# A hybrid decoder trunk on one core: the state-space mixer's tables, its input products and its accumulators

## The chip, the cores and the metric

The kernel runs on one core of a Trainium2 chip. The metric is the device time of one execution in microseconds (us). Engines are named as in the profile: PE is TensorE (PEld its weight loads), DVE is VectorE, ACT is ScalarE, POOL is GpSimd, SP is SyncE, which issues most of the DMAs.

## The reference

The input is x, 256 tokens of width 2048, in float32. Two layers follow each other, and each is a mixer and a gated MLP with a causal convolution of width 3, both behind an RMSNorm and both added to the residual. Layer 0's mixer is a chunked spatial gate. Layer 1's mixer, which the change touches, is a diagonal complex state-space model:

```
u = (rms_norm(h) @ b_w_in)                  # 128 heads of 16 channels
h_t = A h_(t-1) + B u_t ;  y_t = Re(C h_t) + d * u_t      # A diagonal, complex, 64 states a head
ga, gb = split(gelu(y) @ b_w_glu) ;  h = h + ga * sigmoid(gb)
```

## The kernel before

All large products are float32 split in two halves (wh and wl), three products for each. A weight tile (1 MB) is fetched by SP (L108) into one of three raw buffers, cut in pieces of 1024 columns, cast by ACT (wh, L124) and subtracted by DVE (wl, L125) into five buffers each. PE takes them in the order of the list of tiles. Accumulators (acc, accb) come from a PSUM pool of three buffers of two banks each; a second pool, misc, has two buffers of one bank for everything else. Together they fill PSUM.

The scheduler sets the order on each engine by a simulated timeline: it takes, at the time at which the engine is free in it, the instruction earliest in the program among those whose inputs are there. On the chip every engine then runs its instructions in that order, and waits where an input is late. SP does so for its DMAs too.

The mixer's stage lies from about 1046 to 1376 us. PE first makes u = h W (form_a, L786 and L787), eight groups of 256 channels with two weight tiles each, then the GLU's products (group_b, L893 to L895). Between the tiles a step of a software pipeline is put in (step, called once a tile), which takes 16 sets s of eight heads through the state space:

- evac of a group (L1207, L1209, L1213): ACT copies half of acc to t, DVE adds, scales and turns it to u; SP writes u to DRAM (send, L543).
- load and load1, one step ahead of the drive: SP fetches u back as ubd, two blocks of 64 partitions on the diagonal of a tile that is zero elsewhere (L551), the drive's weights pw (L556) and the phase tables tab (cos and sin, 2 x 512 columns, L566). Both halves of tab, partitions 0 to 63 and 64 to 127, hold the same rows of DRAM and are fetched twice.
- drive (L584): four matmuls of 128 x 128 columns, from pw and ubd, into ps_x, a misc buffer.
- take (L597 to L600): ACT copies ps_x crosswise to x, DVE multiplies by the tables. scan (L608 to L610): the recurrence on DVE. turn (L620 to L625): back with the tables, to sp.
- outputs (L639, L645): matmuls on two column tiles of 64, into ps_y. gelu (L653) on ACT, then SP writes y (L655); POOL fetches it as yt (L661); finish casts it (L1168, L1169) to the GLU's stationary operand.

A set's steps come at fixed slots (N_OF): 3, 4, 6 to 14 without a gap, then every second slot up to 24. At slot n the drive, at n + 1 take and scan, at n + 2 turn, at n + 3 outputs.

A pool's memory is given to the next pool when it closes (SBUF: L527, L531 and L534 are the first writes of the mixer's pool).

Of the kernel before, what the change touches and what calls it, by code (L numbers as in the profile page):

```python
# [9 lines left out]
F32 = mybir.dt.float32  # L10
# [3 lines left out]
ALU = mybir.AluOpType  # L14
PSUM = bass.MemoryType.PSUM
DRAM = bass.MemoryType.DRAM

P = 128
# [13 lines left out]
def dram(ap, offset, dims):  # L32
    return bass.AP(ap.tensor, ap.offset + offset, dims)
# [41 lines left out]
class Weights:  # L75


    def __init__(self, nc, pool, tiles):
        self.nc, self.pool, self.tiles = nc, pool, tiles
        self.raw, self.halves = {}, {}  # L80
        self.n_dma = self.n_split = self.n_get = 0
        self.units = []
        for i, (segs, nk, width) in enumerate(tiles):
            for o in range(0, nk * width, 1024):
                self.units.append((i, o, min(1024, nk * width - o)))
        self.first_unit = {}
        for u, (i, o, n) in enumerate(self.units):
            self.first_unit.setdefault(i, u)
# [428 lines left out]
class S5Tokens:  # L517


    def __init__(self, tc, pool, psum, scr, rho, emit):  # L520
        self.nc, self.pool, self.psum = tc.nc, pool, psum
        self.scr, self.rho, self.emit = scr, rho, emit
        self.u, self.st = {}, {}
        self.ubd, self.sp = [], []
        for i in range(4):
            t = pool.tile([P, 4, P], F32, name=f"ubd{i}", tag=f"ubd{i}")
            self.nc.gpsimd.memset(t, 0.0)  # L527
            self.ubd.append(t)
        for i in range(2):
            t = pool.tile([P, 8, 64], F32, name=f"sp{i}", tag=f"sp{i}")  # L530
            self.nc.gpsimd.memset(t, 0.0)  # L531
            self.sp.append(t)
        self.rt = pool.tile([P, 8, 64], F32, name="rt")
        self.nc.gpsimd.memset(self.rt, 0.0)  # L534
# [24 lines left out]
    def load1(self, s):  # L559

        rd = self.scr[3]
        tab = self.pool.tile([P, 2, 512], F32, name=f"tab{s}", tag="tab", bufs=3)
        lh = 8 * s % 64
        o = ((lh // 16) * P + 64 * (s // 8)) * 2048 + (lh % 16) * 64
        for i in range(2):
            self.nc.sync.dma_start(tab[64 * i : 64 * i + 64], dram(rd, o, [[2048, 64], [1024, 2], [1, 512]]))  # L566
        self.st[s]["tab"] = tab

    def load2(self, s):
# [9 lines left out]
    def drive(self, s):  # L579

        st = self.st[s]
        st["x"] = self.psum.tile([P, 512], F32, name=f"ps_x{s}", tag="misc")
        for i in range(4):
            self.nc.tensor.matmul(  # L584
                st["x"][:, i * P : (i + 1) * P], st["pw"][:, i, :], st["ubd"][:, i, :], start=True, stop=True
            )

    def take(self, s):

        nc, pool = self.nc, self.pool  # L590
        V, A = nc.vector, nc.scalar
        st = self.st[s]
        ps = st["x"]
        q = pool.tile([P, 512], F32, name=f"q{s}", tag="q", bufs=2)
        x = pool.tile([P, 512], F32, name=f"x{s}", tag="x", bufs=2)
        cos, sin = st["tab"][:, 0, :], st["tab"][:, 1, :]
        A.copy(x[0:64], ps[64:128])  # L597
        A.mul(x[64:128], ps[0:64], -1.0)
        V.tensor_tensor(q, ps, cos, op=ALU.mult)
        V.tensor_tensor(x, x, sin, op=ALU.mult)  # L600
        st["q"], st["dx"] = q, x

# [66 lines left out]
def tile_hybrid_trunk(  # L669
# [7 lines left out]
    V, A, T, G = nc.vector, nc.scalar, nc.tensor, nc.gpsimd  # L677
# [2 lines left out]
    const = ctx.enter_context(tc.tile_pool(name="const", bufs=1))  # L680
    dpool = ctx.enter_context(tc.tile_pool(name="scratch", bufs=1, space=DRAM))
    wpool = ctx.enter_context(tc.tile_pool(name="weights", bufs=1))
    acc_ps = ctx.enter_context(tc.tile_pool(name="acc_ps", bufs=3, space=PSUM))
    misc_ps = ctx.enter_context(tc.tile_pool(name="misc_ps", bufs=2, space=PSUM))


    def ffn_groups(l):
# [52 lines left out]
    rho = const.tile([P, NH], F32, name="rho")  # L740
# [6 lines left out]
    scr = []  # L747
# [156 lines left out]
    def group_b(*args):  # L904
        for _ in group_b_steps(*args):
            pass
# [101 lines left out]
    with ExitStack() as sgu_ctx:  # L1008
        sp = sgu_ctx.enter_context(tc.tile_pool(name="sgu", bufs=1))
# [69 lines left out]
        for g in range(4):  # L1079
            st = {}  # L1080
# [77 lines left out]


    tmp[0] = ("t", 1)  # L1160
    with tc.tile_pool(name="s5", bufs=1) as sp:

        Ys = [None] * KC

        def emit(s, yt):
            g, yv = Gt[s], yt.rearrange("p (j k) -> p k j", j=4)
            hi, lo = (g[:, i * NT : (i + 1) * NT].rearrange("p (k j) -> p k j", j=4) for i in range(2))
            A.copy(hi, yv)  # L1168
            V.tensor_tensor(lo, yv, hi.bitcast(F32), op=ALU.subtract)  # L1169
            Ys[s] = g  # L1170

        s5 = S5Tokens(tc, sp, misc_ps, scr, rho, emit)
        rbv = rbc.rearrange("p (k j) -> p j k", j=4)
        sched = {}

        def at(slot, fn, *a):
            sched.setdefault(slot, []).append((fn, a))

        for s in range(KC):
            n = N_OF[s]  # L1180
            at(n - 1, s5.load, s)
            at(n - 1, s5.load1, s)
            at(n, s5.drive, s)
            at(n + 1, s5.take, s)
            at(n + 1, s5.scan, s)
            at(n + 1, s5.load2, s)
            at(n + 2, s5.turn, s)
            at(n + 3, s5.outputs, s)
            at(n + 4, s5.gelu, s)
            at(n + LAT[0], s5.fetch, s)  # L1190
            at(n + LAT[1], s5.finish, s)
        order = (
            s5.gelu, s5.take, s5.finish, s5.fetch, s5.turn, s5.scan, s5.outputs, s5.drive, s5.load2, s5.load, s5.load1
        )

        n_slot = [0]

        def step():
            for fn, a in sorted(sched.pop(n_slot[0], []), key=lambda e: order.index(e[0])):
                fn(*a)  # L1200
            n_slot[0] += 1

        for gi in range(8):

            def evac(p, ps, gi=gi):
                t = sp.tile([P, 2, NT], F32, name="t", tag="t", bufs=tmp[0][1])
                A.copy(t, ps[:, :, NT:])  # L1207
                z = sp.tile([P, 2, NT], F32, name="z", tag="z", bufs=2)
                V.tensor_tensor(z, ps[:, :, :NT], t, op=ALU.add)  # L1209
                for i in range(2):  # L1210
                    s = 2 * gi + i
                    u = s5.new_u(s)
                    V.tensor_tensor(u, z[:, i].rearrange("p (k j) -> p j k", j=4), rbv, op=ALU.mult)  # L1213
                    s5.send(s)

            after = {i: step for i in range(2)}
            if gi == 0:
                after[0] = lambda: (drain(2), make_rbc(sp), step())
            form_a(X, [8, 8], [0, 128], evac, after)

        kept = {}

        def glu_keep(i):


            def evac(ps):
                kept[i] = [const.tile([P, 512], F32, name=f"kept{i + a}", tag=f"X{i + a}", bufs=1) for a in range(2)]
                for a in range(2):
                    A.copy(kept[i][a], ps[:, a, :])

            return evac

        def glu_evac(i):
            def evac(ps):
                for a in range(2):
                    z = sp.tile([P, 512], F32, name="z", tag="z", bufs=2)
                    V.tensor_tensor(z, ps[:, a, :], kept[i][a], op=ALU.add)
                    A.activation(z[:, NT:], z[:, NT:], AF.Sigmoid)
                    V.tensor_tensor(z[:, :NT], z[:, :NT], z[:, NT:], op=ALU.mult)
                    hv = hn[:, a, i * P : (i + 2) * P]  # L1240
                    V.tensor_tensor(hv, hv, z[:, :NT], op=ALU.add)
                    square_sum(sp, hv, nss[:, a, i // 2 : i // 2 + 1])
                pending.append(lambda: stage_pair(i // 2, cols[:, 3]))
                if i == KC - 2:
                    total_r(nss, 8, rtok)

            return evac

        fa = group_b_steps(Ys, [4, 4], glu_keep(0))
        fb = group_b_steps(Ys, [4, 4], glu_keep(2))  # L1250
        for f in (fa, fb, fa, fb):
            next(f)
            step()
        for f in (fa, fb):
            for _ in f:
                pass
        for i in range(4, KC, 2):
            group_b(Ys, [4, 4], glu_keep(i), {0: step, 1: step})
        assert not sched
        craw = fetch_conv(sp, 1)  # L1260
        for i in range(0, KC, 2):
            group_b(Ys, [4, 4], glu_evac(i), {1: (lambda: place_conv(craw))} if i == 0 else None, 8)


    tmp[0] = ("a", 2)
    with tc.tile_pool(name="ffn1", bufs=1) as fpool:
        fg = fpool.tile([P, D], F32, name="fg")
        nc.gpsimd.dma_start(fg, dram(final_g, 0, [[0, P], [1, D]]))
        oss = fpool.tile([P, 2, 4], F32, name="oss")
# [62 lines left out]
```

## Time and profile before

| | us |
|---|---|
| median of three runs (lowest, highest) | 2120.24 (2118.4, 2120.79) |
| the profiled execution, its span | 2121.23, 2119.5 |
| PE busy | 2090.7 (99%) |
| PE weight loads busy | 1736.8 (82%) |
| DVE, ACT, POOL busy | 1439.0 (68%), 1134.6 (54%), 90.3 (4%) |
| chain that ended last | PE 95%, DMA 3%, DVE 1% |
| bytes moved | 438.59 MB, mean 207 GB/s |

The busy shares are read against the chain: an engine's busy time counts only where the chain of work that ended last runs over it. PE's busy time is modelled, since matmuls overlap: a matmul of 512 columns is shown as 392 ns long, while the next starts 0.23 us after it. So the distance from start to start is the cost, and the length is not. [...] A DMA's time is from its issue to its landing and holds the time in the queue.

### The profile page before, as it was taken

What the parts mean: (1) busy time and instruction counts of PE and PEld (TensorE: products, weight loads), DVE (VectorE), ACT (ScalarE), POOL (GpSimd) and SP (SyncE); (2) the same over time, 40 slices, a digit from 0 to 9 for tenths busy, and PEclk for the clock granted to TensorE, in tenths of its full rate; (3) what the DMA queues carried; (4) which work ended last, traced back from release to release, by engine and by line L of the source; (5) the groups of instructions that cost most, each with busy time, mean ns of one, the idle gap of its engine ahead of it and who ended that gap; (6) DMA issues with size and microseconds to landing.
All of it is one profiled execution on the core that took longest, in us unless ns stands there. A gap on an engine that the chain in (4) does not pass through costs nothing.

```text
span 2119.5 us, 27328 instructions
## 1 busy us (share of the span) xinstructions
PE 2090.7 (99%) x10279; PEld 1736.8 (82%) x10279; DVE 1439.0 (68%) x2123; ACT 1134.6 (54%) x1656; POOL 90.3 (4%) x142
## 2 busy tenths in 40 slices
PE   9999999999999999999998999999999999999998
PEld 7888888888888788888887788888888888888886
DVE  5476777886896645888788766766555656546665
ACT  6544456554555544555556556655544555445553
POOL 1010000000111110000000000000000000000000
PEclk9999999999999999999999999999999999999999
DMA  8655556666777666565799986565556555565553
GB/s 279 201 180 179 187 192 199 212 236 225 217 241 238 214 213 191 184 223 202 233 263 260 273 269 206 179 211 185 172 194 201 188 182 187 190 197 181 193 183 120
DMA packets 358597, 438.59 MB, mean 207 GB/s; under 512 B 31712, under 2 KB 275520, under 8 KB 357824
## 3 DMA queue, kind: packets, MB, share of 16 engines
q1 hardware_dynamic: 349008, 407.94, 60.5%
q0 software_dynamic: 9424, 28.88, 4.6%
q8 instruction: 81, 1.33, 0.3%
q14 instruction: 52, 0.43, 0.1%
q10 hardware_dynamic: 32, 0.01, 0.0%
HBM read 414.66 MB, written 22.02 MB: 206 GB/s over the span
## 4 chain that ended last, share of the span: by engine, by line
PE 95%; DMA 3%; DVE 1%; ACT 0%; SPq 0%; issue 0%; ACTq 0%; DVEq 0%; POOLq 0%
PE accb L893 26%; PE accb L894 26%; PE accb L895 26%; PE acc L786 4%; PE acc L787 2%; PE zt L916 2%; PE accv L987 1%; PE accv L988 1%; PE accv L989 1%; DMA w<-in_b_w_glu_dram 1%; PE pt L821 1%; DMA w<-in_b_w_in_dram 1%; DMA tab<-rd 1%; DMA ubd<-ud 0%; PE ps_x L584 0%; DMA ud<-u 0%
## 5 line engine op out<-in xcount | busy, mean ns | idle before, releaser
L125 DVE TENSOR_TENSOR wl<-w,wh 128x1024 fp32r<-128x1024 f32 (+1 forms) x721 | 879.4, 1222 | 581.2 <-ACT wh L124 577.9
L124 ACT CAST wh<-w 128x1024 fp32r<-128x1024 f32 (+1 forms) x721 | 754.1, 1050 | 744.5 <-PE accb L895 608.5
L895 PE MATMUL accb<-wh,X 128*128 128x512 f32 x1408 | 552.8, 393 | 0.0
L893 PE MATMUL accb<-wh,X 128*128 128x512 f32 x1408 | 552.1, 392 | 0.0
L894 PE MATMUL accb<-wl,X 128*128 128x512 f32 x1408 | 549.5, 390 | 0.0
L893 PE MATMUL accb<-wh,Gt 128*128 128x512 f32 x1060 | 415.8, 392 | 0.0
L895 PE MATMUL accb<-wh,Gt 128*128 128x512 f32 x1060 | 414.3, 391 | 0.0
L894 PE MATMUL accb<-wl,Gt 128*128 128x512 f32 x1060 | 414.2, 391 | 0.0
L895 PEld LDWEIGHTS accb<-wh,X 128*128 128x128 f32 x1408 | 264.4, 188 | 56.8
L894 PEld LDWEIGHTS accb<-wl,X 128*128 128x128 f32 x1408 | 264.6, 188 | 54.5
L893 PEld LDWEIGHTS accb<-wh,X 128*128 128x128 f32 x1408 | 264.5, 188 | 53.7
L893 PEld LDWEIGHTS accb<-wh,Gt 128*128 128x128 f32 x1060 | 199.2, 188 | 41.6
L895 PEld LDWEIGHTS accb<-wh,Gt 128*128 128x128 f32 x1060 | 199.2, 188 | 41.5 <-issue 0.2
L894 PEld LDWEIGHTS accb<-wl,Gt 128*128 128x128 f32 x1060 | 199.3, 188 | 41.1 <-issue 0.2
L786 PE MATMUL acc<-X,wh 128*128 128x512 f32 x512 | 184.0, 402 | 0.0
L787 PE MATMUL acc<-X,wl 128*128 128x256 f32 x512 | 144.8, 283 | 0.0
L786 PEld LDWEIGHTS acc<-X,wh 128*128 128x128 f32 x512 | 97.2, 190 | 21.8
L924 ACT ACTIVATE a<-zt,conv 128x256 f32<-128x256 f32 x176 | 94.2, 557 | 14.3 <-PE zt L916 8.2
L787 PEld LDWEIGHTS acc<-X,wl 128*128 128x128 f32 x512 | 97.9, 191 | 0.2
L943 ACT ACTIVATE z<-accb,rtok 128x512 f32<-128x512 f32 x88 | 55.7, 684 | 66.5 <-PE accb L895 66.5
L925 DVE SCALAR_TENSOR_TENSOR a<-zt,conv,a 128x255 f32<-128x255 f32 x176 | 77.7, 476 | 13.0 <-ACT a L924 13.0
L928 DVE SCALAR_TENSOR_TENSOR a<-zt,conv,a 128x254 f32<-128x254 f32 x176 | 77.1, 474 | 0.7
(299 smaller groups left out, 1407.3 us busy)
## 6 DMA issues: line engine op xcount, KB each, us to landing
w<-in_f_w_up_dram SPq DMA_DIRECT2D x352, 512.0 KB, 4.6
w<-in_f_w_down_dram SPq DMA_DIRECT2D x80, 1024.0 KB, 5.2
w<-in_b_w_glu_dram SPq DMA_DIRECT2D x64, 512.0 KB, 5.1
w<-in_a_w_in_dram SPq DMA_DIRECT2D x28, 1024.0 KB, 5.3
w<-in_a_w_out_dram SPq DMA_DIRECT2D x16, 1024.0 KB, 5.1
w<-in_b_w_in_dram SPq DMA_DIRECT2D x16, 1024.0 KB, 7.9
w<-in_f_w_down_dram SPq DMA_DIRECT2D x16, 512.0 KB, 3.7
tab<-rd SPq DMA_DIRECT2D x32, 256.0 KB, 6.7
```

Of the source, the lines that this page charges most:

```text
L124: self.nc.scalar.copy(hi[:, a:b], raw[:, o + a : o + b])
L125: self.nc.vector.tensor_tensor(lo[:, a:b], raw[:, o + a : o + b], hi[:, a:b].bitcast(F32), op=ALU.subtract)
L786: T.matmul(ps, wh, Xt[k], start=k == k_first, stop=False, skip_group_check=True)
L787: T.matmul(ps[:, NT:], wl, Xt[k][:, :NT], start=False, stop=k == ktot - 1, skip_group_check=True)
L893: T.matmul(ps[:, tt, :], xh, wh, start=k == k_first, stop=False)
L894: T.matmul(ps[:, tt, :], xh, wl, start=False, stop=False)
L895: T.matmul(ps[:, tt, :], xl, wh, start=False, stop=k == ktot - 1)
L916: T.transpose(pt[:, v * NT + tt * P : v * NT + (tt + 1) * P], z[:, tt, v * NT + q * P : v * NT + (q + 1) * P], ident,)
L924: A.activation(a[:, v], zt, AF.Identity, bias=cw[:, 3, cv : cv + 1], scale=cw[:, 2, cv : cv + 1])
L925: V.scalar_tensor_tensor(a[:, v, 1:], zt[:, : NT - 1], cw[:, 1, cv : cv + 1], a[:, v, 1:], ALU.mult, ALU.add)
L928: V.scalar_tensor_tensor(a[:, v, 2:], zt[:, : NT - 2], cw[:, 0, cv : cv + 1], a[:, v, 2:], ALU.mult, ALU.add)
L943: A.mul(z[:, tt], ps[:, tt], rtok[:, tt : tt + 1])
```

## The change

Three things are changed, all in the mixer's stage.

1. load1 fetches the tables for partitions 0 to 63 alone, one DMA of 256 KB a set in place of two, and ACT copies them to partitions 64 to 127.
2. The drive uses only the two blocks of ubd that are not zero. Each of its four matmuls becomes two of 64 rows and 64 columns, on two row tiles of the array (tile_position (0, 0) and (64, 0)). The row tiles write to two banks, so ps_x is a buffer of two banks, and take reads it as a view over both.
3. ps_x gets a PSUM pool of its own with one buffer. To make room, the pool of three accumulators is closed before the mixer; in it there are two, and a third pool of three is opened for the second FFN.

```diff
-        for i in range(2):
-            self.nc.sync.dma_start(tab[64 * i : 64 * i + 64], dram(rd, o, [[2048, 64], [1024, 2], [1, 512]]))
+        self.nc.sync.dma_start(tab[:64], dram(rd, o, [[2048, 64], [1024, 2], [1, 512]]))
+        self.nc.scalar.copy(tab[64:], tab[:64])
...
-        st["x"] = self.psum.tile([P, 512], F32, name=f"ps_x{s}", tag="misc")
+        xt = self.xps.tile([P, 2, 512], F32, name=f"ps_x{s}", tag="x")[:, :, :256]
         for i in range(4):
-            self.nc.tensor.matmul(
-                st["x"][:, i * P : (i + 1) * P], st["pw"][:, i, :], st["ubd"][:, i, :], start=True, stop=True
-            )
+            for b in range(2):
+                o = 64 * b
+                self.nc.tensor.matmul(
+                    xt[:, b, i * 64 : i * 64 + 64], st["pw"][o : o + 64, i, :], st["ubd"][o : o + 64, i, o : o + 64],
+                    start=True, stop=True, tile_position=(o, 0),
+                )
+        st["x"] = xt.rearrange("p b (i k) -> p i b k", k=64)
...
-        A.copy(x[0:64], ps[64:128])
-        A.mul(x[64:128], ps[0:64], -1.0)
-        V.tensor_tensor(q, ps, cos, op=ALU.mult)
+        x4, q4, c4 = (t.rearrange("p (i b k) -> p i b k", i=4, b=2) for t in (x, q, cos))
+        A.copy(x4[0:64], ps[64:128])
+        A.mul(x4[64:128], ps[0:64], -1.0)
+        V.tensor_tensor(q4, ps, c4, op=ALU.mult)
...
-    acc_ps = ctx.enter_context(tc.tile_pool(name="acc_ps", bufs=3, space=PSUM))
     misc_ps = ctx.enter_context(tc.tile_pool(name="misc_ps", bufs=2, space=PSUM))
+    acc_ctx = ExitStack()
+    acc_ps = acc_ctx.enter_context(tc.tile_pool(name="acc_ps", bufs=3, space=PSUM))
...
-    with tc.tile_pool(name="s5", bufs=1) as sp:
+    acc_ctx.close()
+    with ExitStack() as s5_ctx:
+        acc_ps = s5_ctx.enter_context(tc.tile_pool(name="acc_s5", bufs=2, space=PSUM))
+        xps = s5_ctx.enter_context(tc.tile_pool(name="x_ps", bufs=1, space=PSUM))
+        sp = s5_ctx.enter_context(tc.tile_pool(name="s5", bufs=1))
...
-    with tc.tile_pool(name="ffn1", bufs=1) as fpool:
+    with ExitStack() as ffn_ctx:
+        acc_ps = ffn_ctx.enter_context(tc.tile_pool(name="acc_f1", bufs=3, space=PSUM))
+        fpool = ffn_ctx.enter_context(tc.tile_pool(name="ffn1", bufs=1))
```

## Rows read from the trace of the kernel before

**Rows 1.** Stretches: us, busy us (instructions) of PE, PEld, DVE, ACT, POOL, clock, DMA, GB/s.
```profile
1125.00:1190.00 65.00, 53.92 (x392) 45.71 (x393) 53.88 (x73) 37.49 (x58) 4.62 (x8) 0.92 1.03 271
1190.00:1262.00 72.00, 72.00 (x443) 58.85 (x442) 52.49 (x63) 44.39 (x66) 3.77 (x7) 1.00 0.97 277
```
**Rows 2.** PE by line and shape, 1045 to 1265: busy, mean ns, idle before, releasers.
```profile
L584 PE MATMUL ps_x<-ubd,pw 128*128 128x128 f32 x128 | 20.1, 306 | 14.5 <-DMA ubd<-ud 12.9 <-DVE q L609 1.1 <-PE acc L787 0.3
```
**Rows 3.** Timeline of PE: start, us, instruction [idle before it, releaser].
```profile
1078.27 1.13 PE L584 MATMUL ps_x<-ubd,pw 128*128 128x128 f32 x8 [2.01 <-DMA ubd<-ud]
...
1131.13 2.04 PE L584 MATMUL ps_x<-ubd,pw 128*128 128x128 f32 x8 [7.20 <-DMA ubd<-ud]
...
1186.52 2.05 PE L584 MATMUL ps_x<-ubd,pw 128*128 128x128 f32 x8 [3.37 <-DMA ubd<-ud]
```
**Rows 4.** Stretches around the three stalls (the clock is third from the end).
```profile
1079.00:1084.50 5.50, 5.20 (x26) 4.62 (x25) 3.18 (x6) 2.34 (x4) 0.00 (x0) 0.69 0.98 287
...
1130.50:1138.00 7.50, 6.87 (x32) 6.20 (x33) 4.26 (x7) 3.03 (x5) 0.54 (x1) 0.72 0.92 266
...
1186.00:1191.00 5.00, 4.48 (x18) 4.00 (x19) 4.05 (x6) 4.16 (x8) 0.56 (x1) 0.66 1.03 318
```
**Rows 5.** Chain of waits in order of time: start, us, what.
```profile
1067.72 7.41 DMA ud<-u
...
1121.26 13.90 DMA w<-in_b_w_in_dram
```
**Rows 6.** DMA, 1045 to 1265: total, then issues with KB each and us to landing.
```profile
DMA packets 67623, 58.42 MB, mean 266 GB/s; under 512 B 19408, under 2 KB 60933, under 8 KB 67605
...
tab<-rd SPq DMA_DIRECT2D x32, 256.0 KB, 6.7
...
pw<-pd SPq DMA_DIRECT2D x16, 256.0 KB, 6.4
```
**Rows 7.** Timeline of SP's issues: start, us, what (x2: two issues).
```profile
1049.40 1.27 SPq L566 DMA_DIRECT2D tab<-rd  x2
...
1091.14 1.18 SPq L566 DMA_DIRECT2D tab<-rd  x2
...
1120.53 0.61 SPq L566 DMA_DIRECT2D tab<-rd  x1
...
1130.54 1.19 SPq L566 DMA_DIRECT2D tab<-rd  x1
...
1166.34 1.17 SPq L566 DMA_DIRECT2D tab<-rd  x2
```
**Rows 8.** Timeline of PE around two drives.
```profile
1102.09 0.64 PE L645 MATMUL ps_y<-sp,qw 128*64 128x64 f32 x16
1102.65 1.16 PE L584 MATMUL ps_x<-ubd,pw 128*128 128x128 f32 x8
...
1212.25 1.05 PE L584 MATMUL ps_x<-ubd,pw 128*128 128x128 f32 x8
1213.06 0.48 PE L893 MATMUL accb<-wh,Gt 128*128 128x512 f32 x1
1213.37 0.40 PE L894 MATMUL accb<-wl,Gt 128*128 128x512 f32 x1
```
**Rows 9.** ACT by line and shape, 1045 to 1265.
```profile
L124 ACT CAST wh<-w 128x1024 fp32r<-128x1024 f32 x57 | 59.5, 1052 | 50.9 <-PE acc L786 23.1 <-DMA w<-in_b_w_glu_dram 19.5 <-DMA w<-in_b_w_in_dram 6.5
```
**Rows 10.** Waits of ACT, 1045 to 1265: us in total, times, longest.
```profile
ACT Gt L1168 <- DMA yt<-yd: 11.3, 4, 6.1
```
**Rows 11.** Timeline of ACT, a cast that waits for its fetch.
```profile
1113.03 0.66 ACT L1168 CAST Gt<-yt 128x256 fp32r<-128x256 f32 x1 [3.54 <-DMA yt<-yd]
```
**Rows 12.** Timeline at the mixer's start and at its end.
```profile
1046.20 1.23 DVE L860 TENSOR_TENSOR hn<-accb,hn 128x1024 f32<-128x1024 f32 x1 [0.35 <-PE accb L895]
...
1048.86 1.97 POOL L527 MEMSET ubd<- 128x512 f32 x4 [9.01 <-ACT junk L837]
...
1370.94 1.29 DVE L1237 TENSOR_TENSOR z<-accb,kept 128x512 f32<-128x512 f32 x2 [0.51 <-PE accb L895]
```

More of the change, by code (lines that the diff above doesn't have):

```diff
@@ L517, with __init__ @@
 class S5Tokens:
-    def __init__(self, tc, pool, psum, scr, rho, emit):
-        self.nc, self.pool, self.psum = tc.nc, pool, psum
+    def __init__(self, tc, pool, psum, xps, scr, rho, emit):
+        self.nc, self.pool, self.psum, self.xps = tc.nc, pool, psum, xps
         self.scr, self.rho, self.emit = scr, rho, emit
@@ L1170, in emit @@
             Ys[s] = g
-        s5 = S5Tokens(tc, sp, misc_ps, scr, rho, emit)
+        s5 = S5Tokens(tc, sp, misc_ps, xps, scr, rho, emit)
         rbv = rbc.rearrange("p (k j) -> p j k", j=4)
```

## The prediction, made before the result was known

> **What bounds the kernel now.** I read the page's slices and shares first: TensorE (PE) is busy 99% of the span, so a change gains only where PE stands still or where PE's own work shrinks. Next came the stretches of the mixer stage, which the change touches [rows 1]: from 1125 to 1190 us PE is busy 53.9 of 65 us, and from 1190 to 1262 it is busy all the time. In both the DMA engines are full (share 1.03 and 0.97). The shapes on PE then say where PE waits: nearly all of it stands before the drive matmuls, L584, 14.5 us in all, 12.9 of it for the fetch of the chunk inputs, ubd [rows 2]. [...] The chain of waits says why: the round trip of u waits 7.4 us for its write, and a weight tile issued at 1121.26 needs 13.9 us to land [rows 5]. The transfers stand in a backlog; in this stage the kernel is bound by SP's DMA queue, through the chunk inputs, and PE pays 14.5 + 5.5 = 20 us at most.
>
> **The tables: half the fetch.** The 32 fetches of 256 KB become 16, 4.2 MB less (16 x 0.262), and at the 266 GB/s that the stretch moves that is 15.8 us of full queue [rows 6]. What arrives at PE is read stall by stall, from the tables issued ahead of each [rows 7]. Ahead of the first stall stand three pairs (1049.4 to 1057.1), so 0.79 MB fall away: 3.0 us, more than the 2.0 of idle. I let stall and slow clock go: 2.0 + 1.7 = 3.7 us. Between the first and the second stall eight fetches are issued (1091.14 to 1120.53; half goes, 1.05 MB, 3.9 us): of 7.2 us 3.3 remain, long enough that I leave the slow clock there. Between the second and the third eight more (1130.54 to 1166.34), again 3.9 us against 3.4: stall and clock go, 5.1 us. Sum: 3.7 + 3.9 + 5.1 = 12.7 us. Ends: nothing (the freed time is taken by something else) and 20 us.
>
> A fetch for 64 partitions could be slower than one for 128. The row nearest says hardly: 256 KB of tab, 64 partitions, land in 6.7 us, 256 KB of pw, 128 partitions, in 6.4 [rows 6]. [...] I take the bytes, and keep the other as a rival.
>
> **The tables: 16 copies on ScalarE (ACT).** The nearest row is the cast of 128x1024, 1.05 us [rows 9]; 64 lanes of the same length should take as long. So 16 x 1.05 = 17 us of ACT, which lies beside PE's work. What matters is that each copy waits on ACT for its own fetch, and what is queued behind it there: the weight casts (wh), x, rs and t (to u) and y, behind which SP's writes of y stand, and behind those the next fetch of ubd. The nearest row is the cast of yt, which waits on ACT for a DMA too: 11.3 us of waiting in the stage [rows 10], over the 16 casts of the code 0.7 each. At that rate the copies take 16 x 1.75 = 28 us of ACT. Ends: 0 us on PE's path (the weight casts have five buffers and run ahead of PE) and 28. One wait for yt, 3.54 us, stands right ahead of an x (L597) that is in the chain of waits [rows 11]; I take one such: 3.5 + 1.05 = 4.6 us of loss.
>
> **The drive on two row tiles.** Four matmuls of 128 columns (8 records) become eight of 64 columns (16 records), alternating between two halves of the array. An undisturbed drive takes 1212.25 to 1213.06, 0.81 us; the nearest group of 16 records of 64 columns on two tiles is the second half of the outputs, 1102.09 to 1102.65, 0.56 us [rows 8]. These are column tiles with weights of 64 columns, so it is a bound from the good side; if the row tiles ran one after the other at the old pace per record, 1.62. I take 0.56 and add 0.1 at the entry, where the array takes up another tiling, and nothing at the exit, which the old drive pays too (the matmul behind it lasts 0.48 against 0.40 for the next one): 0.81 - 0.66 = 0.15 a drive. Ahead of the last stall it only makes a stall longer; four drives lie behind it, 0.5 us of gain with rounding down. Ends: 16 x 0.15 = 2.4 us of gain, and 16 x (1.72 - 0.81) = 15 of loss, of which the four behind the stalls pay 3.6.
>
> The exit costs about 0.1 us in the rows even without a change of tiling [rows 8]. [...]
>
> The new x reads span two banks in runs of 64 columns. No row shows that pattern; I cost it at nothing (bound: the reads of x take twice as long, on ACT and DVE and not on PE). Taking x out of misc ends no wait: its single buffer of its own still has to be freed by q, as the one wait of 1.1 us shows [rows 2].
>
> **The pools.** acc is closed and opened again twice. What a pool change waits for is seen on the SBUF pools: the first memset of the mixer's pool stands on POOL until the last user of the old pool, junk, is through [rows 12]. So the first matmul of the mixer waits until the last residual of the first FFN has read its accumulator (DVE, 1.23 us), and the first of the second FFN until the last z additions are done (1.29 us for the two) [rows 12]. In the kernel before PE goes straight on. With the drain of the last matmul and the signal I estimate 1.5 us each, 3.0 us, on the path. Ends: 0 (only the buffer concerned is waited for, and it is another) and 5, if DVE is late by a split of 1.2 us at both. Two accumulators instead of three: a group is two tiles long, and its buffer is wanted again only a whole group later; nothing, as long as ACT isn't blocked that long.
>
> **Sum.** The profiled execution took 2121.2 us (span 2119.5). 2121.2 - 12.7 - 0.5 + 3.0 + 4.6 = 2115.6. It lies 1.0 us over the median of the runs, so 2114.6.
>
> **Rivals.** (B) All stalls go and ACT never holds PE: -20 - 2.4 + 3.0, 2101.8, as a median 2100.8. For it: the queue gets back 15.8 us, more than the 14.5 of idle. Against: the stalls are spread, and stall two is longer than the relief ahead of it. (C) Slower: ACT stands still behind the copies. The schedule puts a copy where its fetch is expected, and the fetches land at 6.7 us in a full queue. If all 16 wait as long as the casts of yt that did wait (11.3 over four, 2.8 us [rows 10]), ACT loses 16 x 3.85 = 62 us; with a third of it at PE, 20.5 us: 2121.2 - 12.7 - 0.5 + 3.0 + 20.5 = 2131.5, as a median 2130.5. It decides from 10 us on, when three of the 16 copies stand in the way of t, x or y. For it: u, ud and ubd are a chain with one slot of slack, and t is on ACT; against: ACT has 28 of 72 us free between 1190 and 1262 [rows 1]. (D) The change doesn't do what it says: the fetch for 64 partitions frees no time, or the weight prefetch takes it up at once. The stalls stay, the pools cost 3.0: 2121.2 - 0.5 + 3.0 = 2123.7, as a median 2122.7. [...]
>
> **How the numbers follow.** Forecast 0.45, B 0.13, D 0.22, C 0.20. The forecast's own range is 2108 to 2120 (relief and ACT 4 to 6 us either way). About 0.2%, 4.2 us, is what a measurement can tell from no change: faster is below 2116.0, slower above 2124.5. Faster: 0.36 of the forecast, all of B, 0.05 of D, 0.54. Same: 0.09 of the forecast, 0.14 of D, 0.01 of C, 0.24. Slower: 0.19 of C and 0.03 of D, 0.22. The range leaves 0.06 of B below 2102 and 0.10 of C above 2130.
>
> **What will show it.** Right: the stalls ahead of L584 are 6 us or less in all and the clock stays up behind the first and the third; tab is issued 16 times; the drive takes about 0.66 us; PE has a gap of about 1.5 us at the first acc and the first accb of the second FFN; the waits of ACT for tab stay below 20 us. Wrong: the copies' waits show up in the chain of waits between t, u and ud or before y (C); or PE still waits 12 us for ubd at full DMA share (D); or a drive is longer than 0.9 us.

## The result, and the profile after

The changed kernel takes 2138.73 us (median of four, 2137.94 to 2141.04), the kernel before in the same comparison 2120.0: a ratio of 1.0091, interval 1.0074 to 1.0109. It is 18.7 us slower where 2114.6 was forecast, outside the range and on the other side. The profiled execution took 2138.98 us (span 2137.3). From the last matmul of the first FFN (the gated MLP of a layer) to the first of the second, the two timelines give 324.97 us before (1045.77 to 1370.74) and 341.66 after (1047.26 to 1388.92): 16.7 of the loss lie in the mixer's stage.

The same stretches as in [rows 1], after (busy us of PE, PEld, DVE, ACT, POOL, then the mean clock granted to PE as a share of the full clock, DMA, GB/s), and three short ones for the clock:

```profile
1125.00:1190.00 65.00, 56.11 (x455) 47.59 (x453) 53.63 (x71) 44.98 (x66) 2.68 (x5) 0.92 0.89 241
1190.00:1262.00 72.00, 68.15 (x438) 54.72 (x437) 51.37 (x63) 45.33 (x66) 5.16 (x9) 0.98 0.78 237
1142.00:1148.00 6.00, 5.58 (x33) 4.83 (x34) 6.00 (x9) 4.01 (x6) 0.54 (x1) 0.72 0.94 249
1156.00:1162.00 6.00, 6.00 (x22) 5.11 (x21) 4.99 (x7) 3.69 (x6) 0.54 (x1) 0.55 0.66 175
1235.00:1240.00 5.00, 5.00 (x28) 4.02 (x26) 4.96 (x7) 4.20 (x7) 0.00 (x0) 0.66 0.34 100
```

The DMA engines are no longer full (0.89 and 0.78 against 1.03 and 0.97), and yet PE is not busier over the two stretches together (124.3 us against 125.9); its clock still falls, in other places (0.72, 0.55 and 0.66 in the three short stretches). What PE waits for has changed, by shape, 1045 to 1280 (the stage is longer now; the rows before end at 1265), to set beside [rows 2]:

```profile
L586 PE MATMUL ps_x<-ubd,pw 64*128 64x64 f32 x256 | 19.5, 286 | 12.5 <-DVE q L604 12.2 <-DMA ubd<-ud 0.3
```

The wait for the chunk inputs is gone (12.9 to 0.3 us), and a wait for q, the product that frees the drive's buffer, has taken its place (1.1 to 12.2). DMA totals and issues in the same stretch, beside [rows 6]:

```profile
DMA packets 65792, 54.71 MB, mean 233 GB/s; under 512 B 19167, under 2 KB 61149, under 8 KB 65773
...
pw<-pd SPq DMA_DIRECT2D x16, 256.0 KB, 6.0
tab<-rd SPq DMA_DIRECT2D x16, 256.0 KB, 5.2
```

ACT by shape, the new copy, and its longest waits in that stretch (us, times, longest), beside [rows 9, 10]:

```profile
L566 ACT COPY tab<-tab 64x1024 f32<-64x1024 f32 x16 | 16.7, 1045 | 28.2 <-DMA tab<-rd 27.5 <-DVE q L604 0.7
```

```profile
ACT Gt L1178 <- DMA yt<-yd: 27.9, 11, 6.7
ACT tab L566 <- DMA tab<-rd: 27.5, 13, 6.3
```

[rows 10] end at 1265 and leave out the longest wait of all. Over 1045 to 1280 the kernel before waits for yt, too:

```profile
ACT Gt L1168 <- DMA yt<-yd: 18.1, 5, 6.8
```

The chain of waits from 1040 to 1290, summed by line, says what sets the end of the stage, first before (the view ends this line short), then after:

```profile
by line: PE accb L893 13.1%; PE accb L894 13.0%; PE accb L895 13.0%; PE acc L786 9.8%; DMA w<-in_b_w_glu_dram 6.0%; DMA w<-in_b_w_in_dram 5.6%; PE acc L787 4.9%; DMA tab<-rd 4.8%; DMA ubd<-ud 4.0%; PE ps_x L584 3.8%; DMA ud<-u 3.0%; issue 2
```

```profile
by line: DMA yt<-yd 12.7%; DMA yd<-y 12.3%; DMA tab<-rd 11.2%; issue 7.7%; PE acc L792 7.2%; DVE wl L125 5.2%; DMA w<-in_b_w_glu_dram 4.2%; ACT wh L124 3.5%; PE acc L793 3.4%; DVE q L615 3.3%; DMA pw<-pd 3.0%; SPq L660 1.9%; DVE q L604 1.7%
```

In the lines listed PE had 57.6% of the chain before and has 10.6% now. The chain runs y to DRAM, back as yt, the cast on ACT, and what stands behind that cast; the fetch of tab, behind which the new copy waits, has 11.2%. One place in full, first ACT's timeline, then PE's (idle before and its releaser in brackets):

```profile
1258.47 0.59 ACT L603 ACTIVATE x<-ps_x 64x512 f32<-64x512 f32 x1
1264.15 0.66 ACT L1178 CAST Gt<-yt 128x256 fp32r<-128x256 f32 x1 [5.09 <-DMA yt<-yd]
1264.71 1.05 ACT L124 CAST wh<-w 128x1024 fp32r<-128x1024 f32 x1
...
1278.85 0.65 ACT L1178 CAST Gt<-yt 128x256 fp32r<-128x256 f32 x1 [6.70 <-DMA yt<-yd]
1279.41 1.04 ACT L124 CAST wh<-w 128x1024 fp32r<-128x1024 f32 x1
```

```profile
1267.78 0.50 PE L900 MATMUL accb<-wl,Gt 128*128 128x512 f32 x1 [1.47 <-DVE wl L125]
...
1280.50 0.50 PE L899 MATMUL accb<-wh,Gt 128*128 128x512 f32 x1 [0.48 <-ACT wh L124]
1281.76 0.50 PE L900 MATMUL accb<-wl,Gt 128*128 128x512 f32 x1 [0.76 <-DVE wl L125]
```

ACT stands still for 5.1 and 6.7 us at a cast whose fetch hasn't landed, a weight cast is queued behind it, and PE runs out of weights for 0.5 to 1.5 us. Last, PE around an undisturbed drive, beside [rows 8], and around the two changes of pools:

```profile
1219.28 0.39 PE L901 MATMUL accb<-wh,Gt 128*128 128x512 f32 x1
1219.60 1.11 PE L586 MATMUL ps_x<-ubd,pw 64*128 64x64 f32 x16
1220.63 0.50 PE L899 MATMUL accb<-wh,Gt 128*128 128x512 f32 x1
1220.97 0.39 PE L900 MATMUL accb<-wl,Gt 128*128 128x512 f32 x1
```

```profile
1047.26 0.39 PE L901 MATMUL accb<-wh,Gt 128*128 128x512 f32 x1
1048.97 0.65 PE L827 MATMUL pt<-ident,hn 128*128 128x128 f32 x4 [1.32 <-DVE hn L866]
...
1387.06 0.39 PE L901 MATMUL accb<-wh,Gt 128*128 128x512 f32 x1
1388.92 0.47 PE L899 MATMUL accb<-wh,X 128*128 128x512 f32 x1 [1.47 <-ACT z L1248]
```

The profile shows each matmul of the drive as two records, so eight of them as x16. From start to next start the drive takes 1.03 us (0.81 before); at the pool changes 1.71 and 1.86 us lie between two starts that are 0.23 apart otherwise.

### The profile page after: what moved, and what is told of

It is laid out like the page before. It is cut to its first block, busy times and chain, and to the rows that moved or that the text cites. A ratio compares the mean times of both kernels' runs of the same rounds, so it can differ in the third digit from the quotient of the medians.

```text
span 2137.3 us, 27557 instructions
## 1 busy us (share of the span) xinstructions
PE 2099.8 (98%) x10407; PEld 1739.0 (81%) x10407; DVE 1440.0 (67%) x2123; ACT 1151.1 (54%) x1672; POOL 90.3 (4%) x142
## 4 chain that ended last, share of the span: by engine, by line
PE 87%; DMA 6%; DVE 3%; ACT 2%; issue 1%; SPq 1%; ACTq 0%; DVEq 0%; POOLq 0%
PE accb L899 24%; PE accb L900 24%; PE accb L901 24%; PE acc L792 4%; PE acc L793 2%; PE zt L922 2%; DMA yt<-yd 1%; DMA yd<-y 1%; PE accv L993 1%; PE accv L994 1%; PE accv L995 1%; DMA tab<-rd 1%; DVE wl L125 1%; PE pt L827 1%; ACT wh L124 1%
## 5 line engine op out<-in xcount | busy, mean ns | idle before, releaser
L899 PE MATMUL accb<-wh,X 128*128 128x512 f32 x1408 | 551.9, 392 | 1.5 <-ACT z L1248 1.5
L901 PE MATMUL accb<-wh,X 128*128 128x512 f32 x1408 | 552.3, 392 | 0.0
L899 PE MATMUL accb<-wh,Gt 128*128 128x512 f32 x1060 | 416.7, 393 | 2.4 <-ACT kept L1239 1.7
L901 PE MATMUL accb<-wh,Gt 128*128 128x512 f32 x1060 | 414.1, 391 | 0.0
L901 PEld LDWEIGHTS accb<-wh,X 128*128 128x128 f32 x1408 | 264.3, 188 | 57.0
L899 PEld LDWEIGHTS accb<-wh,X 128*128 128x128 f32 x1408 | 264.4, 188 | 55.6 <-ACT z L1248 1.9
L899 PEld LDWEIGHTS accb<-wh,Gt 128*128 128x128 f32 x1060 | 199.3, 188 | 45.5 <-ACT kept L1239 1.8
L901 PEld LDWEIGHTS accb<-wh,Gt 128*128 128x128 f32 x1060 | 199.4, 188 | 41.8
L930 ACT ACTIVATE a<-zt,conv 128x256 f32<-128x256 f32 x176 | 94.2, 557 | 14.5 <-PE zt L922 8.2
```

The costliest lines, as they stand in the source:

```text
L899: T.matmul(ps[:, tt, :], xh, wh, start=k == k_first, stop=False)
L901: T.matmul(ps[:, tt, :], xl, wh, start=False, stop=k == ktot - 1)
L930: A.activation(a[:, v], zt, AF.Identity, bias=cw[:, 3, cv : cv + 1], scale=cw[:, 2, cv : cv + 1])
```

## The experiments

Ratios are to the kernel before in the same comparison. Kernels of different comparisons are set against each other by these ratios, 0.001 being 2.1 us; each is good to 0.001 or 0.002, so a difference of two of them to 2 to 4 us.

**e1, the tables alone.** The drive and the pools stay as before.

```diff
-        for i in range(2):
-            self.nc.sync.dma_start(tab[64 * i : 64 * i + 64], ...)
+        self.nc.sync.dma_start(tab[:64], ...)
+        self.nc.scalar.copy(tab[64:], tab[:64])
```

> The kernel before with the tables alone changed: one fetch of 64 partitions a set, and the copy on ACT; the drive, misc and three accumulators as before. Theory ACT (each copy waits on ACT for its own fetch, so that x and q of take come late and the next drive waits for q): slower than before by 4 to 12 us, 2124 to 2132, ACT waits for tab of over 20 us in all, and drives that wait for q instead of ubd. Theory pools (the copies are harmless, the two new pools cost the time): the relief of the DMA queue is left alone, 2106 to 2114, ACT waits for tab under 20 us, stalls ahead of the drive under 6 us.

Measured: 2111.51 us, 0.996 (0.9947 to 0.9972): faster by 9.3. Relief less copies had been forecast at -12.7 + 4.6 = -8.1. So the tables alone gain in spite of ACT's copies, and the loss comes with the other two parts. PE by shape in e1, 1045 to 1265:

```profile
L584 PE MATMUL ps_x<-ubd,pw 128*128 128x128 f32 x128 | 17.5, 280 | 2.4 <-issue 1.7 <-DMA ubd<-ud 0.7
```

**e2, the pools alone**, the drive as before in one of the two banks, beside the change's three pools.

```diff
-        st["x"] = self.psum.tile([P, 512], F32, name=f"ps_x{s}", tag="misc")
+        st["x"] = self.xps.tile([P, 2, 512], F32, name=f"ps_x{s}", tag="x")[:, 0, :]
```

> The pools alone: ps_x in a pool of its own with one buffer, two accumulators in the mixer, pools closed and opened; the drive (four matmuls of 128 columns) and the double fetch of the tables as before. Theory pools: 2128 to 2134, drives wait for q in sum for over 8 us. Theory ACT: only the two changes of pool cost, 1.5 us each, 2121 to 2125, and drives wait for ubd as before, 10 us or more.

Measured: 2122.58 us, 1.0011 (1.0002 to 1.0021): 1.8 us slower. PE by shape in e2:

```profile
L584 PE MATMUL ps_x<-ubd,pw 128*128 128x128 f32 x128 | 18.7, 290 | 11.6 <-DMA ubd<-ud 8.5 <-DVE rs L624 1.7 <-DVE q L599 1.3
```

**e3, pools and row tiles**: the changed kernel with the fetch of before.

```diff
-        self.nc.sync.dma_start(tab[:64], ...)
-        self.nc.scalar.copy(tab[64:], tab[:64])
+        for i in range(2):
+            self.nc.sync.dma_start(tab[64 * i : 64 * i + 64], ...)
```

> The changed kernel without the change of the tables (both halves fetched, no copy on ACT): pools and row tiles. Row tiles longer (a drive starts to ends in 1.04 us in the changed kernel, 0.81 to 0.91 before): 2 to 5 us over the kernel with the pools alone where drives are on the path. Theory ACT: 2123 to 2129. Theory pools: 2131 to 2137.

Measured: 2133.52 us, 1.0063 (1.0051 to 1.0076). The row tiles add 10.9 us to the pools even without the copies. Against this kernel the tables, a gain by themselves, cost: the changed kernel lies 0.0028, 5.9 us, above it.

**e4, pools and tables**, the drive as before.

```diff
-        xt = self.xps.tile([P, 2, 512], ...)[:, :, :256]
+        st["x"] = self.xps.tile([P, 2, 512], ...)[:, 0, :]
...
-            for b in range(2):
-                ...
+            self.nc.tensor.matmul(st["x"][:, i * P : (i + 1) * P], st["pw"][:, i, :], st["ubd"][:, i, :], start=True, stop=True)
```

> The changed kernel without the row tiles: pools and tables, the drive as four matmuls of 128 columns. If the row tiles cost 2 to 5 us: 2134 to 2137. Theory ACT: as slow as the tables alone plus 3 us for the pools. Theory pools: 2122 to 2128, since relief and pools' cost come together.

Measured: 2119.32 us, 0.9994 (0.9985 to 1.0003), less than any of the three expectations. So the pools cost 7.8 us on top of the tables, and the row tiles 0.0097 of the time, about 20 us, on top of both. The row tiles are the larger part. ACT's waits for yt in e4, 1045 to 1280:

```profile
ACT Gt L1173 <- DMA yt<-yd: 32.3, 9, 8.4
```

They are as long as in the changed kernel (27.9 us), with the old drive.

**e5, the cast in its place.** The changed kernel; the cast of a finished tile keeps its place in the program's order on ACT.

```diff
-            A.copy(hi, yv)
+            tc.keep_in_program_order(A.copy(hi, yv))
```

> The changed kernel whole, but the cast of each finished token tile (the ACT instruction that waits for yt, at the line of Gt) is issued where the program names it and not moved ahead of the weight casts. Theory 'ACT': in the changed kernel ACT stands at these casts for yt (27.9 us in 11 waits, mean of the long ones 6.7), the weight casts queue behind and TensorE loses them; then 10 us or more go, 2138.7 falls to 2128 or less. Theory 'row tiles': the time is lost on TensorE itself at the drives and what follows them; then the cast's place is worth 3 us at most, 2136 to 2140.

Measured: 2125.24 us, 1.0023 (1.0013 to 1.0032): 13.5 us (14.4 by the ratios) back from the place of one instruction a tile, with the order on PE unchanged. The theory "ACT" holds for more than half of the loss. PE's wait at the drive (1045 to 1280), ACT's wait for yt and the chain by line (1040 to 1290):

```profile
L586 PE MATMUL ps_x<-ubd,pw 64*128 64x64 f32 x256 | 18.4, 279 | 8.9 <-DVE q L604 8.9
```

```profile
ACT Gt L1178 <- DMA yt<-yd: 3.0, 2, 2.8
```

```profile
by line: DMA tab<-rd 15.1%; PE accb L899 14.3%; PE accb L900 13.4%; PE accb L901 13.3%; PE acc L792 7.5%; issue 5.2%; PE acc L793 3.6%; PE ps_x L586 2.7%; DMA yd<-y 2.0%; DMA pw<-pd 1.9%; DVE rs L629 1.7%; PE ps_y L644 1.6%; DVE q L628 1.6%
```

yt is out of the lines listed, yd is down to 2.0%, and the GLU's matmuls (L899 to L901) have 41%.

**e6, half the fetch by columns, no copy.**

```diff
-  dma_start(tab[64 * i : 64 * i + 64], dram(rd, o, [[2048, 64], [1024, 2], [1, 512]]))
+  dma_start(tab[64 * i : 64 * i + 64, :, :256], dram(rd, o, [[2048, 64], [1024, 2], [1, 256]]))
...
-  cos, sin = st["tab"][:, 0, :], st["tab"][:, 1, :]
+  cos, sin = (st["tab"][:, i, :256].rearrange(...).to_broadcast([P, 2, 256]) for i in range(2))
...
```

> The kernel before with only the fetch of the tables cut: each of the two transfers takes the first 256 of the 512 columns (so the second 256 columns are multiplied by the tables of the first: this part of the computation is changed), the same bytes as after the change, on all 128 partitions, with no copy on ACT. If the 12.7 us of relief were right and the copies on ACT cost the 4.6 us forecast, this gives 2120.8 - 12.7 = 2108. If the copies cost nothing, it gives the 2111.5 of the tables alone. If the gain of the tables alone came from the number of transfers or from the partitions and not from the bytes, it stays near 2120.

Measured: 2107.1 us, 0.9937 (0.9924 to 0.995): 13.7 us of relief (12.7 forecast). With the copies, in e1, it was 4.4 us less (4.6 forecast).

**e7, two buffers of one bank for the drive**, from e4.

```diff
-        st["x"] = self.xps.tile([P, 2, 512], ...)[:, 0, :]
+        st["x"] = self.xps.tile([P, 512], ...)
...
-        xps = s5_ctx.enter_context(tc.tile_pool(name="x_ps", bufs=1, space=PSUM))
+        xps = s5_ctx.enter_context(tc.tile_pool(name="x_ps", bufs=2, space=PSUM))
```

> Tables and pools of the change, the drive as before (one 128-row matmul per group), and the drive's PSUM pool with two buffers of one bank in place of one of two banks. Theory 'one buffer': a drive that waits for the product of the drive before it (q, 3.3 us with the one buffer) is what makes the pools cost on top of the tables (2111.5 to 2119.3); then this falls to 2113 to 2116. Theory 'accumulators': the cost is the two accumulators in place of three for the mixer; then it stays at 2118 to 2121.

Measured: 2118.53 us, 0.9988 (0.9979 to 0.9998). Not told apart from e4: the single buffer isn't it.

**e8, a longer drive**, from e4.

```diff
+            for _ in range(i < 2):
+              self.nc.tensor.matmul(...)   # the same matmul once more
```

> Tables and pools of the change, the drive as before but with its first two matmuls issued twice: 0.4 us more of TensorE in each of 16 drives, 6.4 us in all, the result the same. Theory 'the stage amplifies': a drive longer by some tenths of a us moves the order and the buffers of the whole stage and costs twice its own time or more; then 2119.3 rises to 2133 to 2139, as with the row tiles. Theory 'only its own time': it rises to 2125 to 2127, and the row tiles lose their 19.4 us by something of their own (entry, exit, pauses between the two row tiles, the strided reads).

A drive of e8, from its start to the next matmul:

```profile
1213.14 0.38 PE L584 MATMUL ps_x<-ubd,pw 128*128 128x128 f32 x2
...
1214.40 0.48 PE L898 MATMUL accb<-wh,Gt 128*128 128x512 f32 x1
```

That is 1.26 us against 0.81, so 0.45 x 16 = 7.2 us more, a little over the 6.4 expected. Measured: 2133.05 us, 1.0054 (1.0041 to 1.0068): 13.7 us more than e4 (12.7 by the ratios) for these 7.2 us of matmuls. The stage amplifies a longer drive, whether or not it lies on row tiles. ACT's waits for yt are no longer than in e4 (32.3), so their length doesn't say what they cost:

```profile
ACT Gt L1177 <- DMA yt<-yd: 26.7, 7, 6.0
```

**e9 and e10, e4 and e8 with the cast in its place**, by the diff of e5.

> Tables and pools of the change, the drive as before, and the cast of a finished token tile on ACT left where the program names it. The changed kernel fell by 13.5 us from this (2138.7 to 2125.2). Theory 'the longer drive moves the cast': with the short drive the cast stands well already, so little changes, 2116 to 2120, and what is left between this and 2125.2 (5 to 9 us) is what the row tiles cost by themselves. Theory 'the cast stands wrong in every version': this falls by as much, to 2105 to 2109, and the row tiles cost 16 to 20 us by themselves.

> The longer drive (two matmuls issued twice, 6.4 us of TensorE more in all, the result the same) with tables and pools, and the cast left in its place. Theory 'the longer drive moves the cast': the 13.7 us that the longer drive cost fall to its own 6.4, that is 2123 to 2127 if the short drive pinned takes 2117 to 2120. Theory 'buffers and clock': a longer drive costs twice its time wherever the cast stands, and this stays at 2130 to 2134.

Measured: 2116.57 us, 0.9975 (0.9966 to 0.9985), and 2125.84 us, 1.0025 (1.0015 to 1.0035). The place of the cast is worth 4.0 us with the short drive, 6.1 with the longer one and 14.4 with the row tiles. What is left of the row tiles is 1.0023 - 0.9975, 10 us. The longer drive still costs 0.0050, 10.6 us, and not its own 7.2: the 2125.84 lie within the first theory's range, but that the cast alone amplifies the drive has fallen. An undisturbed drive in e9, and the matmul ahead of it:

```profile
1205.17 0.39 PE L896 MATMUL accb<-wh,Gt 128*128 128x512 f32 x1
1205.40 1.05 PE L584 MATMUL ps_x<-ubd,pw 128*128 128x128 f32 x8
```

Clock and DMA share, 1080 to 1200, first e9, then the changed kernel with the cast in place (e5):

```profile
1080.00:1200.00 120.00, 111.09 (x824) 95.10 (x823) 104.69 (x139) 89.03 (x128) 6.78 (x12) 0.97 0.98 267
```

```profile
1080.00:1200.00 120.00, 108.25 (x860) 91.28 (x857) 99.73 (x132) 81.80 (x117) 6.24 (x11) 0.94 0.91 250
```

**e11, the tables alone, the copy right ahead of its use, the cast in its place** (the diff of e5 too).

```diff
-        self.nc.scalar.copy(tab[64:], tab[:64])          # load1
...
+        self.tc.keep_in_program_order(A.copy(st["tab"][64:], st["tab"][:64]))    # take
```

> The tables alone, with the copy on ACT issued right ahead of its use (behind the drive, where the table has long landed) and the cast of a finished tile left in its place; pools and drive as before. If ACT's waits for the tables (18.3 us in 9) and for yt (22.6 us in 7) are what the half fetch without copies saved over the tables alone (2107.1 against 2111.5), this gives 2105 to 2109. If the copies' own 16 x 1.05 us on ACT cost it, it stays at 2110 to 2113.

Measured: 2110.55 us, 0.9951 (0.9938 to 0.9964). The fastest kernel that leaves nothing out, but told apart neither from e1 (0.996) nor, by the intervals, from e6 (0.9937). Whether the place of the copy matters stays open.

**e12 and e16, one row tile, and the two tiles in turn of four** (a single time each).

```diff
-                o = 64 * b
+                o = 0                       # e12
...
-        for i in range(4):
-            for b in range(2):
+        for b in range(2):                  # e16
+            for i in range(4):
```

> The changed kernel with both halves of the drive on the first row tile (the second half then takes the inputs of the first, so this part of the computation is changed): the same 16 matmul records to a drive. If the two row tiles run beside each other in the changed kernel, a drive now gets longer, from 1.03 us to 1.6 us or more, from its start to the next matmul. If they run one behind the other anyway, it stays at 0.95 to 1.1 us.

> The changed kernel with the four matmuls of the first row tile ahead of the four of the second, in place of one of each in turn. If the two tiles run beside each other only when neighbours in the order lie on different tiles, the drive goes from 1.03 us to near the 1.92 of one row tile (two neighbours remain, so 1.6 to 1.9). If the hardware looks further ahead, it stays at 1.0 to 1.2.

An undisturbed drive in e12 and in e16:

```profile
1221.04 2.00 PE L586 MATMUL ps_x<-ubd,pw 64*128 64x64 f32 x16
1222.96 0.50 PE L899 MATMUL accb<-wh,Gt 128*128 128x512 f32 x1
```

```profile
1204.24 1.60 PE L586 MATMUL ps_x<-ubd,pw 64*128 64x64 f32 x16
1205.77 0.50 PE L899 MATMUL accb<-wh,Gt 128*128 128x512 f32 x1
```

1.92 and 1.53 us against 1.03: the row tiles do run beside each other, best where neighbours lie on different tiles. e16 fits neither expectation. It has one place where neighbours change the tile, and saves 0.39 us, more than three records of 0.12, so the second tile starts well before the first has ended. The single times are 2139.43 and 2137.84 us: 0.9 and 0.5 us more in each drive cost the changed kernel nothing that shows. With the early cast it is not bound by PE.

**e13 and e14, two and three accumulators**, from e4, the drive in the misc pool.

```diff
-        st["x"] = self.xps.tile([P, 2, 512], ...)[:, 0, :]
+        st["x"] = self.psum.tile([P, 512], F32, name=f"ps_x{s}", tag="misc")
...
-        acc_ps = s5_ctx.enter_context(tc.tile_pool(name="acc_s5", bufs=2, space=PSUM))
-        xps = s5_ctx.enter_context(tc.tile_pool(name="x_ps", bufs=1, space=PSUM))
+        acc_ps = s5_ctx.enter_context(tc.tile_pool(name="acc_s5", bufs=3, space=PSUM))    # e13: 2
```

> Tables of the change, and of its pools only the two accumulators: the drive goes into the small pool as before and there is no pool of its own. Theory 'accumulators': two in place of three cost 7.8 us, and this stays at 2118 to 2121. Theory 'drive's buffer': the pool of the drive costs it, and this falls to the 2111.5 of the tables alone, at most 2114. Theory 'change of pools': the two gaps where the old pool is closed and the new one opened, and the order that follows, cost it; then this and the run with three accumulators both stay at 2116 to 2120.

> As the run before it, but with three accumulators in the new pool, as the kernel before has: only the change of pools is left. Theory 'accumulators': 2111.5 plus the 3.0 forecast for the two changes, 2112 to 2115. Theory 'change of pools': 2116 to 2120, as with two.

Measured: 2121.72 us, 1.0 (0.9991 to 1.0009), and 2120.47 us, 0.9999 (0.999 to 1.0008). Neither the number of accumulators nor the drive's own buffer matters; closing one pool and opening another is enough to cost the 8 us on top of the tables. PE in e14, beside e1:

```profile
L584 PE MATMUL ps_x<-ubd,pw 128*128 128x128 f32 x128 | 19.3, 297 | 7.5 <-DVE q L599 3.3 <-DMA ubd<-ud 3.3 <-ACT y L653 0.5
```

**e15, the kernel before with the cast in its place**, by the diff of e5.

> The kernel before with the cast of a finished tile left where the program names it. Theory 'early cast': what the cast costs is small where the drive is short, as it was with tables and pools (2.8 us); 2116 to 2121. Theory 'the cast stands wrong everywhere': it falls by 7 or more, to 2114 or less.

Measured: 2122.35 us, 1.0004 (0.9994 to 1.0013): no change, and just above the range of the first theory. The cast's place does no harm there.

**e17, e12 with the cast in its place**, by the diff of e5.

> Both halves of the drive on the first row tile (the second half then takes the inputs of the first, so this part of the computation is changed), and the cast of a finished tile left where the program names it. The drive takes 1.92 us in place of 1.03: 0.89 x 16 = 14.2 us more of TensorE. Theory 'with the cast in place TensorE is the bound': the 2125.2 us of the changed kernel with the cast in place rise by 10 to 16, to 2135 to 2141, where with the early cast the same change cost nothing. Theory 'slack': the drives wait for the product of the drive before anyway (8.9 us in that kernel), so at most a third shows, 2125 to 2130.

Measured: 2128.75 us, 1.0041 (1.0029 to 1.0053): 3.8 us over e5 for 14.2 us of drives; "slack" holds. The drives' wait for q fell from 8.9 us (e5) to this:

```profile
L586 PE MATMUL ps_x<-ubd,pw 64*128 64x64 f32 x256 | 33.2, 281 | 2.9 <-DVE q L604 2.9
```

## Why the prediction was wrong, step by step

The parts, by the ratios: tables -8.5 us (e1), pools on top +7.2 (e4 less e1), row tiles with the cast in place +10.2 (e5 less e9), and the cast 14.4 - 4.0 = +10.4 more than without them. That is +19.3, the ratio of 1.0091. The parts depend on the order in which they are added: the tables give -8.5 alone, -3.6 on top of the pools (e4 less e2) and +5.9 on top of pools and row tiles (the changed kernel less e3). The sum of the prediction took them as independent. The row tiles cost 10 us or more in each pair of kernels that differ in them: 11.0 (e3 less e2), 20.6 (the changed kernel less e4) and 10.2 (e5 less e9), where a gain of 0.5 was put in.

- **What bounds the kernel: right.** SP's queue did it. With half the fetch the waits for ubd fell from 12.9 us to 3.6 (e6, 1045 to 1265), and e6 gained 13.7 us. This is the kernel before; with the change another path bounds it. The terms for the clock in the prediction (1.7 us at the first and at the third stall, 5.5 in all) are estimates from [rows 4], each a stretch's length times what its clock lacks to 1; no run shows one of them by itself. From 1125 to 1190 the clock is 0.92 before, 1.00 in e1 and 0.97 in e6, by the same estimate 5.2, 0 and 2.0 us.
- **The tables' relief, -12.7: right** (13.7). **The copies, +4.6: right in size for the tables alone**, if the 4.4 between e1 and e6 are the copies. 16.7 us of ACT were forecast as 17 (a copy on 64 partitions took 1045 ns, the cast of the same length on 128 in [rows 9] 1052), the waits for tab came to 27.5 us where 11 were put in and below 20 was the mark. Rival C is not the whole of it: e3 has no copy and loses, e1 has all 16 and gains. But it isn't ruled out as a part: tab stands in the chain with 11.2% (15.1% in e5), and the +5.9 of the tables on top of pools and row tiles are not explained otherwise. No run has the changed kernel with half the fetch and no copy. Rival C's mechanism was near in another way, too: ACT did stand still behind another instruction, the cast of yt. [rows 10, 11] had shown it, with 11.3 us of waiting to 1265; to the end of the stage it was 18.1.
- **The pools, +3.0: half right.** The two gaps came, 1.71 and 1.86 us where 0.23 is usual, 3.1 together, as forecast; what share of them the end of the last matmul and the signal have is shown by no run. The whole was 1.8 us alone and 7 to 8 on top of the tables. In e1 the drives wait 2.4 us in all, in e14, with the change of pools and nothing else, 7.5: the 5.1 between them and the 3.1 of the gaps make 8.2. That the sum comes out may be chance: the clock over 1080 to 1200, 1.00 in e1, is 0.96 in e14, up to 4.8 us more, and other waits differ. Of the 7.2, 4.0 went when the cast was put in its place (e9). In e2 that wait is 11.6 us, below the 14.5 of before, so there was nothing more to lose. The scheduler laid another order after the change of pools, and the gain of the tables came partly from where it had put the drives in e1. That the order is what does it is read from the traces; no run held the order and changed the pool.
- **The drive on two row tiles, -0.5: this step failed, and it turned the sign.** Three things were wrong in it. (1) The pace: 0.56 us was taken from a group on column tiles, 0.07 for a pair of records, one on each tile; the nearest row had weights of 64 columns, and the row tiles' have 128. Measured was 1.03, 0.13 a pair (that the weights are the reason wasn't tested), with 0.32 us from the matmul ahead (0.23 for the old drive, in e9; 0.09 more, where the author's estimate for the entry was 0.1, and no run shows what takes it) and 0.34 behind it (0.31): 1.69 against 1.35, a loss of 0.34 x 16 = 5.4 us where 0.15 a drive was to be gained. The bad end of that term, 1.62 us for records one after the other at the old pace, was too low as well: on one tile they take 1.92 (e12). (2) Only four drives were counted, since a drive in a stall was to cost nothing; that much is borne out by e17, where most of a longer drive vanished in the wait for q. (3) The order on the engines and the slack in it were taken as fixed. The cast of yt stands on ACT ahead of x, rs and the weight casts, where its fetch hasn't landed: 27.9 us of waiting, 18.1 before. Leaving it in place gave 13.5 us back (e5), and gave nothing in the kernel before (e15). The wait by itself is not the work of the row tiles, for e4 has 32.3 us of it and there the cast's place is worth 4.0; with the row tiles a wait of about that length costs 14.4. What makes it dearer isn't shown.
- **What stays open:** of the 10 us that the row tiles cost with the cast in place, 5.4 are the drives themselves. The clock (0.94 against 0.97 over 120 us, up to 3.6 us) and PE's waits from 1040 to 1400 (15.5 us against 12.4) are read from the profiles of e5 and e9, and no run separates them. Why the first tenths of a us in a drive cost more than they take (e10, where the clock is 1.00 over the same 120 us), and the next 0.9 us less (e17), isn't settled. The 4.4 us between e1 and e6 may be the copies, their place or the 64 partitions.
- **The signs named beforehand:** tab is issued 16 times and the pool gaps are there (right); the waits for ubd are below 6 us, but the stalls ahead of the drive, which the sign named, are 12.5 in all (wrong); the clock was to stay up behind two of the old stalls, which are gone, and it fell elsewhere (0.55 from 1156 to 1162); the waits for tab were to stay below 20 us and didn't; a drive longer than 0.9 us was named as wrong, and it came.

Rival D, by which the fetch for 64 partitions frees no time, was not borne out: e1 gained 9.3 us. Whether 64 partitions slow a single fetch is not shown: in e1 tab's 256 KB landed in 6.4 us and the 256 KB of pw, for 128 partitions, in 5.6; in the changed kernel it was 5.2 and 6.0.

## What to carry to other kernels

Where a scheduler lays the order on the engines, an edit of some tenths of a us on one engine can move an instruction of another one; compare the two orders before pricing the edit, and look at what stands behind each instruction that waits for a DMA. Parts of a change that use the same slack can't be priced one by one and added: the tables were worth -8.5 us alone and +5.9 on top of the rest. A cast that waits for a round trip is best held behind work whose inputs are there (13.5 us in e5, nothing in e15). And count the records before splitting a matmul over row tiles: halving 128 columns doubled their number, from 8 to 16, and gave back less than that (0.81 us a drive before, 1.03 on two tiles and 1.92 on one).

## What the runs showed of the hardware

- Matmuls on two row tiles of 64 overlapped most when neighbours in the order lay on different tiles: 16 records took 1.03 us alternating, 1.53 in two groups of eight, 1.92 on one tile. In the groups they overlapped in part, 0.39 us of the 1.92 (e16 against e12). How far the tiles ran beside each other depended on the order.
- A record of 64 columns on one tile cost 1.92 / 16 = 0.12 us, one of 128 columns on the whole array 0.81 / 8 = 0.10: half the columns saved nothing.
- Reading ps_x in runs of 64 columns from two banks cost nothing: ACT's copy took 583 ns (584 before), DVE's product 690 (690).
